# Transposing the attention values of the second mixer: from four TensorE transposes to a write, reads and one VectorE transpose of 32x32 blocks

## The chip, the cores and the metric

The kernel runs on one core of a Trainium2 chip. The metric is the time of one execution on the device in microseconds (us), lower is better. The engines are TensorE (PE in the profile; its weight loads are PEld), VectorE (DVE), ScalarE (ACT), GpSimd (POOL) and SyncE (SP), which only issues transfers. Each has its own queue and works through it in order; they meet at semaphores.

## The reference

The program is a two-layer encoder trunk on 512 tokens of width 1024. Layer 0 has an mLSTM mixer, layer 1 a band attention, and each has a memory attention beside it and a gated channel mixer behind it. The change is in layer 1. What it computes, cut down:

```python
ks_, vs_ = jnp.split(rmsnorm(x, kv_norm_g) @ w_kv, 2, axis=-1)   # 768 + 768 columns
q, q_mem = jnp.split(rmsnorm(x, norm_mix_g[1]) @ b_w_in, [768], axis=-1)
# 12 heads of 64; a chunk of 64 queries sees its own chunk and the 8 before it
s = jnp.einsum('bqhd,bkhd->bhqk', qc, kc) * 64 ** -0.5 + bias     # -inf where not valid
p = jax.nn.softmax(s, axis=-1)
out = jnp.einsum('bhqk,bkhd->bqhd', p, vc)
mem_out = memory_attention(q_mem, mem, mem_w_kv[1])               # 4 heads, 256 memory rows
x = x + jnp.concatenate([out, mem_out], axis=-1) @ b_w_out
```

With 512 tokens (8 chunks) the band of 9 chunks reaches every earlier token, so each query sees all tokens up to the end of its own chunk.

## The kernel before

Activations are held with channels on the 128 partitions and the 512 tokens along the free axis. A float32 product is done as three products of parts: every operand is split into a high part (a copy by ScalarE, L147) and a low part (a subtraction by VectorE, L148), and `mm3` (L203 to L205) adds high by high, high by low and low by high in PSUM.

The twelve heads go in six pairs, and one pair fills the 128 partitions. `project_pair(j)` (L1477) makes what pair j needs. It projects the values, the keys and the queries one after the other (`project`, eight steps of three products each, 24 products of 512 columns). The values and keys are scaled by the row of reciprocal norms (`times_row`, L1480), the queries by L652. The keys go through `head_keys` (L612, L613), the queries through `head_queries` (L602 to L606), where GpSimd clears half of each low part with a memset (L602).

The values are needed the other way round, with tokens on partitions, because they are the stationary operand of the last product of the attention. Before, TensorE transposes the four blocks of 128x128 into one PSUM bank (L1491), and two splits of 128x256 read that bank and write the parts for tokens 0 to 255 and 256 to 511.

`band_attention(j)` then goes through four blocks of 128 queries: scores on TensorE (L622), the sum with the bias and its minimum on VectorE (L1518), exponential on ScalarE (L1522), reciprocal and scaling on VectorE (L1523, L1524), transposes of the probabilities on TensorE (L1533) and their split. At its end come the products with the values (L1554 and L1555).

`weave` emits the steps of the attention of pair j between the steps of the projections of the pairs that come later, at a rate written by hand for each attention, so that TensorE has products to do while a softmax is on its way:

```python
for j in range(4):
    until(lambda: j in qkv, fill)
    weave(band_attention(j, *qkv.pop(j)), fill, (1.68, 1.826, 1.633, 1.848)[j], 4)
```

After pair 3 come the memory attention, pair 4, a second memory attention and pair 5, in the same manner. In other parts of the program the order on TensorE, ScalarE and VectorE is written out by hand. Here it isn't: the framework's planner takes the instructions in the order in which they were emitted as their priority, estimates with its own costs when each could start, and lays down the order of every queue, those of SyncE and GpSimd too. Buffers come from rings with a fixed number of places, and an instruction that writes a new buffer waits until a place is free. The rings that matter are `wr` (3 raw weight tiles, filled by SyncE's loads, L162), `wh0` to `wl2` (3 pairs of split weights), `t` (8 tiles of 128x512, for scaled values, softmax results and the like), `fh` and `fl` (4 each, for the split values of pairs 0 to 4), `u` (50), and in PSUM `mm` (3 banks, for projections and, before, the transposed values), `sc` (3) and `tr` (2).

The last stage of the kernel already turns a tensor in the way that the change does: `load_quadrants` (L1603) reads a stored tensor in pieces so that blocks of 32x32 lie ready, and `token_major` (L1611) transposes these blocks on VectorE.

Of the kernel before, what the change touches and what calls it, by code (L numbers as in the profile page):

```python
# [9 lines left out]
F32 = mybir.dt.float32  # L10
# [6 lines left out]
P = 128  # L17
D = 1024
S = 512
KT = D // P  # L20
TT = S // P
# [27 lines left out]
UNITS = {PLAIN + i: tuple((i, j) for j in range(*LOADS[i][2:])) for i in range(len(LOADS))}  # L49

H = S // 2
ORDERED = {mybir.EngineType.PE, mybir.EngineType.Activation, mybir.EngineType.DVE}


def f(ap):
    return ap.bitcast(F32)
# [3 lines left out]
def trunk(  # L60
# [18 lines left out]
    nc = tc.nc  # L79
    V, A, G = nc.vector, nc.scalar, nc.gpsimd  # L80
# [12 lines left out]
    dram = ctx.enter_context(tc.tile_pool(name="dram", bufs=1, space=bass.MemoryType.DRAM))  # L93

    def sb(tag, shape, dtype=F32):
        count[0] += 1
        return pool.tile(shape, dtype, tag=tag, name=f"{tag}{count[0]}", bufs=bufs[tag])

    def ps(tag):
        count[0] += 1  # L100
        return psum.tile([P, S], F32, tag=tag, name=f"p{tag}{count[0]}", bufs=pbufs[tag])
# [12 lines left out]
    ident = cpool.tile([P, P], F32, name="ident")  # L114
# [31 lines left out]
    def split(hi, lo, src, on_act=True, pinned=False):  # L146
        high = A.copy(hi, src) if on_act else V.tensor_copy(hi, src)  # L147
        low = V.tensor_tensor(out=lo, in0=src, in1=f(hi), op=ALU.subtract)  # L148
        if pinned:
            pin(high)  # L150
            pin(low)
# [42 lines left out]
    def weights(*args):  # L194
        return parts(load(*args))

    def rows(w, c0, n, k0=0, k1=None):
        k1 = k1 if k1 is not None else w.shape[0] // P
        return w[k0 * P : k1 * P, c0 : c0 + n].rearrange("(k p) c -> p k c", p=P)

    def mm3(o, lh, ll, rh, rl, first, last, more=False):

        nc.tensor.matmul(o, lh, rh, start=first, stop=False, skip_group_check=more)  # L203
        nc.tensor.matmul(o, lh, rl, start=False, stop=False, skip_group_check=more)  # L204
        nc.tensor.matmul(o, ll, rh, start=False, stop=last, skip_group_check=more)  # L205

    def project(w, c0, act, tag="mm", parts=None):


        n = len(act)  # L210
        wh, wl = parts or weights(rows(w, c0, P), n, P)
        o = ps(tag)
        for k in range(n):
            mm3(o, wh[:, k, :], wl[:, k, :], act[k][0], act[k][1], k == 0, k == n - 1)
            yield
        return o
# [167 lines left out]
    for k in range(KT):  # L384
        if k % 2 == 0:
            src = mem[:, k * P : (k + 2) * P].rearrange("(m p) c -> p m c", p=P)
# [53 lines left out]
    norm = Norm()  # L440
# [158 lines left out]
    def head_queries(t, scale=1.0):  # L599
        qs, ls = ([sb("u", [P, S], F32R) for _ in range(2)] for _ in range(2))  # L600
        for h, r in enumerate(HEADS):
            G.memset(f(ls[h])[HEADS[1 - h], :], 0.0)  # L602
            A.activation(qs[h][r, :], t[r, :], AF.Copy, scale=scale)
            V.scalar_tensor_tensor(ls[h][r, :], t[r, :], scale, f(qs[h])[r, :], op0=ALU.mult, op1=ALU.subtract)
        for h, r in enumerate(HEADS):
            A.copy(qs[h][HEADS[1 - h], :], f(qs[h])[r, :])  # L606
        return qs, ls

    def head_keys(t):
        ks = [sb("u", [P, S], F32R) for _ in range(2)]  # L610
        for h, r in enumerate(HEADS):
            A.copy(ks[h][r, :], t[r, :])  # L612
            V.tensor_tensor(out=ks[h][HEADS[1 - h], :], in0=t[r, :], in1=f(ks[h])[r, :], op=ALU.subtract)  # L613
        return ks
# [32 lines left out]
    def queries(o, row):  # L647

        if row is None:
            return head_queries(o, HD**-0.5)  # L650
        q = sb("t", [P, S])
        V.scalar_tensor_tensor(q, o, HD**-0.5, row, op0=ALU.mult, op1=ALU.mult)  # L652
        return head_queries(q)
# [89 lines left out]
    class ChannelMixer:  # L743
# [54 lines left out]
        def block_sums(self):  # L798

            self.sums = []  # L800
            for k in range(KT // 2):
# [6 lines left out]
                for o, x, y in (  # L808
                    (ta[:, :H], b1[:, H:], b1[:, :H]),
                    (ta[:, H:], b2[:, H:], ta[:, :H]),  # L810
                    (tb[:, :H], b2[:, H:], b1[:, H:]),
                    (tb[:, H:], b2[:, :H], ta[:, H:]),
                ):
                    V.tensor_tensor(out=o, in0=x, in1=y, op=ALU.subtract)
                yield
                for t in (ta, tb):
                    hi, lo = sb("u", [P, S], F32R), sb("u", [P, S], F32R)
                    split(hi, lo, t)
                    forms += [(hi[:, :H], lo[:, :H]), (hi[:, H:], lo[:, H:])]
                    yield  # L820
# [54 lines left out]
        def products(self, o, w, act, first=False):  # L875

            n = KT // 2
            for k in range(n):
                mm3(o[:, :H], w[0][:, k], w[1][:, k], *act[k], first and k == 0, k == n - 1, True)

# [14 lines left out]
        def tiles(self):  # L895
# [17 lines left out]
            def own_sums():  # L913
                yield
                for part in prep.all_sums():
                    part()
                    yield
# [7 lines left out]
            first = self.forms if self.l else own_sums()  # L925
            with tc.manual_schedule(engines=ORDERED):
                og = run(self.plain_chain(0, False, w[0]))
# [228 lines left out]
    act = acts  # L1156
# [39 lines left out]
    e, u, c, r = (cpool.tile([P, TT, AH], F32, name=f"gate{i}") for i in range(4))  # L1196
# [253 lines left out]
    norm2, kvact, act = Norm(), [], []  # L1450
# [10 lines left out]
    norm = norm2  # L1461
# [15 lines left out]
    def project_pair(j):  # L1477
        def times_row(o):
            t = sb("t", [P, S])
            V.tensor_tensor(out=t, in0=o, in1=norm.row, op=ALU.mult)  # L1480
            return t

        ov = yield from project(w_kv, AW + j * P, kvact)
        t = times_row(ov) if norm.row is not None else None
        o = yield from project(w_kv, j * P, kvact)
        if t is None:
            t = times_row(ov)
        k = head_keys(times_row(o))
        tp = ps("mm")
        for T in range(TT):  # L1490
            nc.tensor.transpose(tp[:, T * P : (T + 1) * P], t[:, T * P : (T + 1) * P], ident)  # L1491
        v = []
        for i in range(2):

            w = sb("u" if j == 5 else ("fh", "fl")[i], [P, S], F32R).rearrange("p (h c) -> p h c", h=4)
            split(w[:, :, :HD], w[:, :, HD:], tp[:, i * MEM : (i + 1) * MEM].rearrange("p (h c) -> p h c", h=4))
            v += [w[:, :2, :], w[:, 2:, :]]
        q = queries((yield from project(b_w_in, j * P, act)), norm.row)
        qkv[j] = q, k, v

    def band_attention(j, q, k, v):
# [88 lines left out]
    for hf in range(2):  # L1590
        G.dma_start(fgb[hf], bass.AP(tensor=final_g.tensor, offset=final_g.offset + hf * S, ap=[[0, P], [1, S]]))
    xt = [[None] * 2 for _ in range(TT)]
    B = 32
    xq = []

    def load_quadrants():

        for hf in range(2):
            xq.append(sb("pt", [P, 5 * S])[:, : 4 * S].rearrange("p (f t) -> p f t", t=P))
            for b in range(4):  # L1600
                block = xspill[4 * hf][:, b * P :]
                src = bass.AP(tensor=block.tensor, offset=block.offset, ap=[[S, B], [B * S, 16], [1, P]])
                tc.keep_in_program_order(nc.sync.dma_start(xq[hf][b * B : (b + 1) * B], src))  # L1603

# [3 lines left out]
    def token_major(T, hf):  # L1608
        xt[T][hf] = sb("u", [P, S])
        block = xq[hf].rearrange("p f (c t) -> p f c t", t=TT)[:, :, :, T]  # L1610
        V.transpose(xt[T][hf].rearrange("p (f c) -> p f c", c=B), block)  # L1611

# [35 lines left out]
    n = LAST // 2  # L1648
# [33 lines left out]
    whole = slice(0, S)  # L1682
    with tc.manual_schedule(engines=ORDERED):
        os_ = [ps(t) for t in ("mm", "mm", "mm", "sc")]
# [93 lines left out]
```

## Time and profile before

| | before |
|---|---|
| median of 3 runs | 1167.95 us (1167.5 to 1168.17) |
| profiled execution, its own time | 1168.55 us |
| span of the profile | 1166.5 us |
| granted clock of TensorE | 0.998 of full speed |
| busy: TensorE, its weight loads | 1156.2 us, 1033.2 us |
| busy: VectorE, ScalarE, GpSimd | 1001.8 us, 747.9 us, 151.2 us |
| the change's stage | about 608 to 798 us of the span |

The span is the time between the first and the last instruction of the profiled execution; the execution's own time has about 2 us around it. Busy time of TensorE counts a product from its start to its modelled end, and products overlap, so the distance between starts says more than a duration. In a row of a timeline the columns are start, duration, engine, line, operation, output and input by tile name, shape and count; a bracket at the end gives how long the engine was idle before it and what ended that. In a row for one line, the three numbers are shortest, median and longest duration in ns. "DMA to landing" is the time from issue to the last byte.

### The profile page before, as it was taken

The numbers are of one execution on the slowest core, as the hardware profiler recorded it, in microseconds if no ns is written. First come the engines' busy times: TensorE is split into PE (matmuls) and PEld (weight loads), VectorE is DVE, ScalarE is ACT, GpSimd is POOL, SyncE is SP. The second block draws the span as 40 slices with busy tenths as digits, with TensorE's granted clock in tenths as the row PEclk, the third lists the DMA queues.
The fourth block names the chain that finished last, engine by engine and source line by source line (L and its number), as shares of the span: only waits on it lengthen the run. The fifth ranks groups of instructions, "written<-read, shape, count | busy, mean of one in ns | idle before, by whom it ended". The sixth has DMA issues, their size and how long they took to land.

```text
span 1166.5 us, 19282 instructions
## 1 busy us (share of the span) xinstructions
PE 1156.2 (99%) x7189; PEld 1033.2 (89%) x7189; DVE 1001.8 (86%) x1781; ACT 747.9 (64%) x1343; POOL 151.2 (13%) x254
## 2 busy tenths in 40 slices
PE   9999999999999999999999999999999999999997
PEld 9988888888999999999888888778899999999986
DVE  6877688779999988888797888898999998889977
ACT  6548677657776655555575667776776665555654
POOL 1211101000122222111021000100010111111100
PEclk9999999999999999999999999999999999999999
DMA  8745325244468878777564322335445767777682
GB/s 282 230 110 134 96 56 153 66 134 140 139 157 182 213 178 195 182 173 162 147 193 133 91 62 63 122 107 157 142 126 143 174 146 180 172 180 174 143 157 78
DMA packets 207855, 171.26 MB, mean 147 GB/s; under 512 B 9256, under 2 KB 182030, under 8 KB 207762
## 3 DMA queue, kind: packets, MB, share of 16 engines
q1 hardware_dynamic: 188018, 123.93, 37.1%
q0 software_dynamic: 19168, 45.06, 19.3%
q8 instruction: 56, 0.92, 0.3%
q10 hardware_dynamic: 576, 1.05, 0.2%
q14 instruction: 37, 0.30, 0.1%
HBM read 133.09 MB, written 40.85 MB: 149 GB/s over the span
## 4 chain that ended last, share of the span: by engine, by line
PE 96%; DVE 2%; ACT 1%; DMA 0%; issue 0%; POOL 0%; POOLq 0%; DVEq 0%
PE pmm L203 19%; PE pmm L204 18%; PE pmm L205 18%; PE ptr L204 6%; PE ptr L203 6%; PE ptr L205 6%; PE psc L203 5%; PE psc L204 5%; PE psc L205 5%; PE psc L622 2%; PE ptr L1533 1%; PE ptr L1554 1%; PE ptr L1555 1%; PE ptr L691 1%; PE pmm L513 0%; PE ptr L705 0%
## 5 line engine op out<-in xcount | busy, mean ns | idle before, releaser
L203 PE MATMUL pmm<-u,wh 128*128 128x256 f32 (+1 forms) x992 | 334.9, 338 | 0.1
L205 PE MATMUL pmm<-u,wl 128*128 128x256 f32 (+1 forms) x992 | 332.1, 335 | 0.0
L204 PE MATMUL pmm<-u,wh 128*128 128x256 f32 (+1 forms) x992 | 331.9, 335 | 0.0
L148 DVE TENSOR_TENSOR wl<-wr,wh 128x1024 fp32r<-128x1024 f32 (+4 forms) x165 | 184.8, 1120 | 56.0 <-ACT wh L147 55.4
L205 PEld LDWEIGHTS pmm<-u,wl 128*128 128x128 f32 x992 | 186.3, 188 | 18.9
L203 PEld LDWEIGHTS pmm<-u,wh 128*128 128x128 f32 x992 | 186.4, 188 | 16.7 <-ACT u L147 0.9
L204 PEld LDWEIGHTS pmm<-u,wh 128*128 128x128 f32 x992 | 186.5, 188 | 16.2 <-DVE u L148 0.5
L147 ACT CAST wh<-wr 128x1024 fp32r<-128x1024 f32 (+4 forms) x165 | 159.6, 970 | 62.5 <-PE pmm L204 30.1
L203 PE MATMUL ptr<-u,wh 128*128 128x512 f32 x272 | 106.5, 392 | 0.0
L204 PE MATMUL ptr<-u,wh 128*128 128x512 f32 x272 | 106.3, 391 | 0.0
L205 PE MATMUL ptr<-u,wl 128*128 128x512 f32 x272 | 105.8, 389 | 0.0
L147 ACT CAST fh<-pt 128x512 fp32r<-128x512 f32 x120 | 74.8, 625 | 34.5 <-DVE pt L1059 33.2
L203 PE MATMUL pmm<-u,fh 128*128 128x256 f32 x320 | 88.8, 278 | 0.0
L205 PE MATMUL pmm<-u,fl 128*128 128x256 f32 x320 | 88.6, 277 | 0.0
L204 PE MATMUL pmm<-u,fh 128*128 128x256 f32 x320 | 88.5, 276 | 0.0
L981 ACT COPY t<-pmm 128x256 f32<-128x256 f32 x120 | 45.0, 375 | 67.3 <-PE pmm L205 67.2
L148 DVE TENSOR_TENSOR fl<-pt,fh 128x512 fp32r<-128x512 f32 x120 | 82.3, 687 | 3.1
L765 DVE SCALAR_TENSOR_TENSOR t<-t,cols,t 128x511 f32<-128x511 f32 x88 | 65.9, 749 | 7.3 <-ACT t L772 5.8
L203 PE MATMUL psc<-u,wh 128*128 128x256 f32 (+1 forms) x208 | 63.2, 304 | 0.0
L205 PE MATMUL psc<-u,wl 128*128 128x256 f32 (+1 forms) x208 | 62.9, 302 | 0.0
L204 PE MATMUL psc<-u,wh 128*128 128x256 f32 (+1 forms) x208 | 62.9, 302 | 0.0
L203 PEld LDWEIGHTS pmm<-u,fh 128*128 128x128 f32 x320 | 60.1, 188 | 2.2 <-ACT t L981 0.7
(359 smaller groups left out, 2642.0 us busy)
## 6 DMA issues: line engine op xcount, KB each, us to landing
wr<-in_ffn_w_up_dram SPq DMA_DIRECT2D x46, 512.0 KB, 8.5
pt<-in_ffn_w_up_dram SPq DMA_DIRECT2D x40, 512.0 KB, 8.3
wr<-in_ffn_w_down_dram SPq DMA_DIRECT2D x32, 512.0 KB, 5.4
wr<-in_a_w_in_dram SPq DMA_DIRECT2D x20, 512.0 KB, 3.8
xspill<-bias POOLq DMA_DIRECT2D x32, 256.0 KB, 7.0
without_row<-bias POOLq DMA_DIRECT2D x24, 256.0 KB, 4.1
wr<-in_w_kv_dram SPq DMA_DIRECT2D x12, 512.0 KB, 4.0
without_row<-t POOLq DMA_DIRECT2D x24, 256.0 KB, 4.1
```

Source lines behind the costliest of these rows:

```text
L147: high = A.copy(hi, src) if on_act else V.tensor_copy(hi, src)
L148: low = V.tensor_tensor(out=lo, in0=src, in1=f(hi), op=ALU.subtract)
L203: nc.tensor.matmul(o, lh, rh, start=first, stop=False, skip_group_check=more)
L204: nc.tensor.matmul(o, lh, rl, start=False, stop=False, skip_group_check=more)
L205: nc.tensor.matmul(o, ll, rh, start=False, stop=last, skip_group_check=more)
L622: nc.tensor.matmul(o, a, b, start=first and i == 0, stop=i == 1)
L691: nc.tensor.transpose(tp[:, a, i, :], es[T2, h][:, i, a * P : (a + 1) * P], ident)
L765: V.scalar_tensor_tensor(acc[:, n:], src[:, : S - n], self.fw[:, c * FT + j : c * FT + j + 1], acc[:, n:], op0=ALU.mult, op1=ALU.add,)
L981: A.copy(o, r[:, :H])
L1533: nc.tensor.transpose(tp[:, b * P : (b + 1) * P], es[T, h][:, b * P : (b + 1) * P], ident)
L1554: nc.tensor.matmul(o2[:, s * P :], w, hi_at(pts[h], s, s, TT - s), start=s == 0, stop=False)
L1555: nc.tensor.matmul(o2[:, s * P :], w, lo_at(pts[h], s, s, TT - s), start=False, stop=s == TT - 1)
```

## The change

The scaled values `t` of pair j are written by GpSimd to a tensor of their own in DRAM, with partition 32a + b going to row 4b + a. After the keys and the queries are emitted, SyncE reads that tensor back in four transfers, one for each group of 32 tokens out of every 128. Such a transfer fills 32 partitions: partition b holds, for each a and each block T of 128 tokens, the 32 values of channel 32a + b, so a piece is 32 numbers, 128 bytes. One instruction of VectorE transposes all the 32x32 blocks and orders them so that tokens lie on the partitions and channels along the free axis. The two splits read this tile in SBUF, and no longer a PSUM bank. They, the reads and the transpose are now emitted after the projection of the queries and not before it. The tiles `r` and `tp` come from the ring `t`; the four TensorE transposes and their bank from `mm` are gone.

```diff
@@ project_pair(j)
         o = yield from project(w_kv, j * P, kvact)
         if t is None:
             t = times_row(ov)
+        vt = dram.tile([P, S], F32, name=f"values{j}")
+        rows4 = bass.AP(tensor=vt.tensor, offset=vt.offset, ap=[[S, 4], [4 * S, B], [1, S]])
+        G.dma_start(rows4, t)
         k = head_keys(times_row(o))
-        tp = ps("mm")
-        for T in range(TT):
-            nc.tensor.transpose(tp[:, T * P : (T + 1) * P], t[:, T * P : (T + 1) * P], ident)
+        q = queries((yield from project(b_w_in, j * P, act)), norm.row)
+        r, tp = sb("t", [P, S]), sb("t", [P, S])
+        for b in range(4):
+            block = vt[:, b * B :]
+            src = bass.AP(tensor=block.tensor, offset=block.offset, ap=[[4 * S, B], [P, 16], [1, B]])
+            nc.sync.dma_start(r[b * B : (b + 1) * B].rearrange("p (n c) -> p n c", c=B), src)
+        V.transpose(
+            tp.rearrange("p (T a c) -> p a T c", T=TT, a=4), r.rearrange("p (a T c) -> p a T c", T=TT, a=4)
+        )
         v = []
         for i in range(2):
             w = sb("u" if j == 5 else ("fh", "fl")[i], [P, S], F32R).rearrange("p (h c) -> p h c", h=4)
             split(w[:, :, :HD], w[:, :, HD:], tp[:, i * MEM : (i + 1) * MEM].rearrange("p (h c) -> p h c", h=4))
             v += [w[:, :2, :], w[:, 2:, :]]
-        q = queries((yield from project(b_w_in, j * P, act)), norm.row)
         qkv[j] = q, k, v
```

`B` is 32; its definition moves to the head of the file, with no other effect.

2 lines of the change are left out of this document (1 added, 1 removed).

## The prediction

> **What bounds the kernel now.** I read the page first, then the windows of the second mixer, then single rows of it.
>
> ```profile
> span 1166.5 us, 19282 instructions
> ...
> PE 1156.2 (99%) x7189; PEld 1033.2 (89%) x7189; DVE 1001.8 (86%) x1781; ACT 747.9 (64%) x1343; POOL 151.2 (13%) x254
> ...
> PE 96%; DVE 2%; ACT 1%; DMA 0%; issue 0%; POOL 0%; POOLq 0%; DVEq 0%
> ```
>
> TensorE is busy for 99% of the span and holds 96% of the chain that ended last, so an instruction taken off TensorE shortens the end unless it makes TensorE wait. VectorE at 86% is the next engine, and it gets the new work. The shares by stage (time, then TensorE matmul, weight load, VectorE, ScalarE, GpSimd, clock, DMA share, GB/s) for the stage that the change touches, cut at the starts of the bands:
>
> ```profile
> 608.40:628.90 20.50, 20.50 (x93) 16.83 (x92) 15.51 (x21) 12.19 (x19) 4.72 (x9) 1.00 0.51 160
> 628.90:653.55 24.65, 24.54 (x129) 20.73 (x128) 21.75 (x56) 16.45 (x39) 2.19 (x4) 1.00 0.31 86
> 653.55:678.80 25.25, 25.25 (x133) 21.09 (x131) 21.53 (x56) 16.63 (x39) 2.30 (x4) 1.00 0.31 88
> 678.80:703.50 24.70, 24.70 (x131) 20.66 (x129) 20.98 (x56) 16.89 (x39) 0.00 (x0) 1.00 0.21 63
> 703.50:738.00 34.50, 34.50 (x174) 28.58 (x173) 27.11 (x65) 23.01 (x49) 3.12 (x6) 1.00 0.34 106
> 738.00:758.50 20.50, 19.78 (x106) 15.79 (x106) 19.54 (x50) 15.44 (x43) 3.13 (x6) 1.00 0.26 80
> 758.50:798.40 39.90, 39.60 (x217) 32.07 (x216) 35.66 (x100) 29.03 (x76) 1.09 (x2) 1.00 0.36 104
> ```
>
> Up to 738 us TensorE idles 0.11 us in all, and VectorE idles 2.9 to 7.4 us in each window. From 738 to 758.5 VectorE idles only 0.96 us and TensorE 0.72 us: there the two are close to joint bounds. The granted clock is 1.00 throughout, so it enters no term.
>
> **Removed: 24 transposes on TensorE, four for each pair of heads.** Their row, and the order of TensorE around the first four:
>
> ```profile
> L1491 PE MATMUL pmm<-ident,t x24: 270/272/273, 619.6 to 744.6; 128*128 128x128 f32 x24
> ...
> 619.12 0.39 PE L204 MATMUL pmm<-u,wh 128*128 128x512 f32 x1
> 619.35 0.39 PE L205 MATMUL pmm<-u,wl 128*128 128x512 f32 x1
> 619.58 0.60 PE L1491 MATMUL pmm<-ident,t 128*128 128x128 f32 x4
> 619.93 0.48 PE L203 MATMUL pmm<-u,wh 128*128 128x512 f32 x1
> 620.25 0.40 PE L204 MATMUL pmm<-u,wh 128*128 128x512 f32 x1
> ```
>
> Starts of products are 0.23 us apart (619.12 to 619.35). Without the four transposes L203 would start at 619.58 and L204 at 619.81; it starts at 620.25, so four transposes cost 0.44 us of the line, not four times 272 ns, since they are pipelined. The gain is 6 x 0.44 = 2.64 us. Its ends: 6 x 0.35 = 2.10 (619.58 to 619.93, the shift of the first start) and 6 x 0.60 = 3.60 (the four as busy time). I take 0.44, which counts the whole delay of the following stream.
>
> The bank of PSUM that the transposes filled comes free as well. With 0.11 us of idle on TensorE before 738 there is nothing for it to repair: 0.
>
> **Added on VectorE: one transpose of 32x32 blocks per pair, 128x512.** The kernel has that instruction in its last stage:
>
> ```profile
> L1611 DVE STREAM_TRANSPOSE u<-pt x8: 1042/1070/1099, 1135.3 to 1146.8; 128x512 f32<-128x512 f32 x8
> ```
>
> So 6 x 1.07 = 6.42 us more on VectorE. What covers it is idle time there. The next windows run, for pairs 1, 2 and 5, from the start of the value projection's scaling (L1480) to about the end of the splits of its transposed values:
>
> ```profile
> 632.20:645.90 13.70, 13.59 (x75) 11.44 (x74) 12.92 (x35) 9.75 (x23) 2.19 (x4) 1.00 0.29 78
> 656.84:671.00 14.16, 14.16 (x75) 11.54 (x74) 13.20 (x35) 9.36 (x22) 2.30 (x4) 1.00 0.37 104
> 740.00:752.00 12.00, 11.61 (x64) 9.00 (x62) 11.76 (x26) 9.11 (x25) 3.12 (x6) 1.00 0.29 97
> ```
>
> In these stretches VectorE idles 0.78, 0.96 and 0.24 us: no room for 1.07. Outside them there is: in band 0, 24.65 - 21.75 - 0.78 = 2.12 us. The question is whether the transpose may wait until then. The rows of the values of pair 1 and of single gaps:
>
> ```profile
> 632.20 0.69 DVE L1480 TENSOR_TENSOR t<-pmm,rb 128x512 f32<-128x512 f32 x1
> 642.34 0.41 DVE L148 TENSOR_TENSOR fh<-pmm,fh 128x256 fp32r<-128x256 f32 x1
> 672.90 0.68 DVE L642 TENSOR_TENSOR t<-ptr,t 64x512 f32<-64x512 f32 x1 [1.27 <-ACT t L641]
> 682.48 1.23 DVE L148 TENSOR_TENSOR wl<-wr,wh 128x1024 fp32r<-128x1024 f32 x1 [1.77 <-ACT wh L147]
> 735.94 1.23 DVE L148 TENSOR_TENSOR wl<-wr,wh 128x1024 fp32r<-128x1024 f32 x1 [3.00 <-ACT wh L147]
> ...
> 670.76 0.50 PE L1554 MATMUL ptr<-pt,fh 128*128 128x512 f32 x1
> ```
>
> The values of pair 1 are scaled at 632.20, split from 642.34, and first used by L1554 at 670.76: 28 us of slack after the split began. The edit also emits transpose and splits after the query projection, so in the planner's order they stand behind work that is due sooner. A gap of 1.27 to 3.00 us holds the transpose whole. I therefore take 0 for pairs 0 to 4 (ends: 0, and 5 x 1.07 = 5.35 if every gap turns out to be needed). For pair 5, in 738 to 758.5, the ends are -0.44 (hidden, gain kept) and +1.07 (all on the line); with 0.96 us idle against 1.07 I take the middle, +0.3, in place of that pair's gain.
>
> The two splits per pair keep their engines and size; only their source moves from PSUM to SBUF. ScalarE's half in either case, in the same shape:
>
> ```profile
> L147 ACT CAST fl<-pmm x5: 372/372/373, 623.8 to 720.2; 128x256 fp32r<-128x256 f32 x5
> L147 ACT CAST u<-wr x2: 400/404/408, 727.4 to 727.7; 128x256 fp32r<-128x256 f32 x2
> ```
>
> That is 32 ns more each, and ScalarE idles 8 us a band: 0.
>
> The Trainium skill (VectorE: DVE Perf Modes, The three transpose paths) gives 390 ns for a 128x128 TensorE transpose in bf16 and 311 ns for VectorE's blocks. Taken at 390 ns each, the 24 would be an estimated 9.4 us; the rows' 0.11 us per transpose decides instead.
>
> **Added on GpSimd and SyncE: six writes and 24 reads.** The nearest rows, first a write of 256 KB from GpSimd with its landing, then the eight reads of the last stage, each 512 pieces of 512 B:
>
> ```profile
> L1460 POOL DMA_DIRECT2D xspill<-fl x4: 539/540/542, 597.1 to 609.4; - x4
> DMA to landing us min/median/max: 2.3/2.5/3.5
> ...
> L1603 SPq DMA_DIRECT2D pt<-xspill x8: 346/858/1706, 1122.4 to 1128.9; - x8
> DMA to landing us min/median/max: 6.4/8.2/8.8
> ...
> wr<-in_w_kv_dram SPq DMA_DIRECT2D x12, 512.0 KB, 4.0
> rep<-maskf POOLq DMA_DIRECT2D x12, 16.0 KB, 3.3
> ```
>
> A new read has 512 pieces of 128 B; none of that size is in the trace. By count of pieces the four reads of a pair (2,048) are half of those eight (4,096); a weight load has 1,024 and lands in 4.0 us, and the small-piece row (64 rows of 256 B) in 3.3. So landing lies between 3.3 and 8.8 us; I take 6.4, the fastest of the like-shaped reads. For pair 1: scaled by 632.9, issue 0.54, write landed 2.5, four issues 4 x 0.37 = 1.5 (a single one in SyncE's rows below), landing 6.4: 643.8. The ends are 632.9 + 0.54 + 2.3 + 1.4 + 3.3 = 640.4 and 632.9 + 0.54 + 3.5 + 6.8 + 8.8 = 652.5. All lie 18 us or more ahead of 670.76.
>
> The queues that these steps stand in:
>
> ```profile
> 634.51 12.96 SPq L162 DMA_DIRECT2D wr<-in_w_kv_dram  x2
> 652.47 0.37 SPq L162 DMA_DIRECT2D wr<-in_b_w_in_dram  x1
> ...
> 637.35 1.15 POOL L602 MEMSET u<- 64x512 f32 x2 [23.08 <-ACT t L1522]
> 662.86 1.10 POOL L602 MEMSET u<- 64x512 f32 x2 [22.69 <-PE psc L622]
> ```
>
> On SyncE the reads wait for the write to land, and weight loads queue behind them. A load fills one of three raw buffers as soon as a split frees it and is itself split three projections later, at least 3 x 24 x 0.23 = 16.6 us, of which it takes 4.0; SyncE waits some 12 us between the two loads of the first row. A hold of 3.5 + 1.5 us is covered: 0; without that cover it would be those 5 us a pair. On GpSimd the write waits for the scaled values, and memsets and bias reads queue behind; GpSimd idles 23 us at a time: 0. If the write stood behind the memset of 662.86 instead, it would issue near 664, and 2.5 + 1.5 + 6.4 + 1.07 + 0.8 (two splits of 0.41) brings the values at 676.3, 5.5 us after 670.76; a planner that orders by readiness puts it ahead, so I price it at 0 too.
>
> Two more buffers of the ring t (8) are held for a while per pair, while the old one comes free when the write has landed. Ends: 0, and one step on a tile of that size late, 0.69 us per pair as in L1480's row; I take 0.
>
> **Sum.** 5 x (-0.44) + 0.3 = -1.9 us. The profiled execution took 1168.55 us (2.05 around its span), 0.60 over the median of the runs shown, 1167.95. The forecast is 1168.55 - 1.9 = 1166.65 for such an execution and 1166.05, say 1166.0, for the median. Its own range is -3.6 (0.60 each) to -0.7 (5 x 0.35 less, 1.07 more): 1164.4 to 1167.3.
>
> **Rivals.**
> - *VectorE becomes the bound.* For it: the 93% or more in the three short windows, and 95% in 738 to 758.5. Against it: gaps of 1.27 to 3.00 us at the ends of the bands in which it waits for others. Price: all 6.42 on the line less 2.64, +3.8: 1171.7.
> - *VectorE stands at the head of its queue waiting for pieces (slower).* Place: the transpose, if it is ordered before its reads have landed; behind it stand that band's softmax steps, on which TensorE's transposes (L1533) wait. At the old place of the splits (642.34) the wait would be 1.5 us by my landing and up to 10.2 by the late end. A band hides 2.12 us, so with a wait w a pair loses 1.07 + w - 2.12 and gains 0.44: it decides from w = 1.5. At w = 3, about half of the middle between those ends, since the order has much room after 642, 6 x 1.51 = +9: 1177. For it: 128-byte pieces are new and the planner's guess of them is not visible; against it: the room.
> - *Nothing is gained*: the freed 0.44 us is taken up by waits of TensorE for softmax results, because filler products run out sooner. For it: the stage is dense on both engines. Against it: TensorE idles 0.11 us before 738. Time: 1167.95.
>
> The Trainium skill (DMA: Bandwidth & Descriptors, Specifications) sets 512 B as the least transfer for line rate and says that smaller ones are done by read-modify-write. By that rule the reads would land toward the late end and the second rival would hold; no transfer of 128-byte pieces has been seen here.
>
> **How the numbers follow.** Forecast 0.48, VectorE as bound 0.20, late pieces 0.15, nothing gained 0.17. A measurement of this kernel tells 0.2% (2.3 us) from no change. The forecast's own range lies on both sides of -2.3: 0.30 of its 0.48 I give to faster, as 0.44 per pair kept in all six is already -2.64; the rest and the nothing-gained case are the same, 0.35; the other two are slower, 0.35. The range goes from 1164.4 to 1174, which takes in VectorE as the bound and late pieces up to w = 2.5, and leaves out the rest of that case and a small part below.
>
> **What would show it.** Right: L1491 gone, matmul starts 0.23 us apart across its places, the transposes of VectorE in gaps after the old splits with no wait on DMA before them, splits done before L1554. Wrong: idle time of VectorE before its transpose that a DMA ends; TensorE idling over 1.2 us in the stage, on L148 or L1524; landings over 10 us; SyncE's weight loads late for ScalarE's L147. A stage before 738 that is longer than before makes the prediction wrong even where the total falls.

## The result and the profile after

The changed kernel takes 1171.62 us (median of 7 runs, 1171.46 to 1171.97) against 1167.98 us (7 runs, 1167.5 to 1168.38) for the kernel before: ratio 1.0032, 95% interval 1.002 to 1.0044. It is slower by 3.6 us, where 1.9 us less had been forecast. The profiled execution took 1171.97 us.

The page of the changed kernel (engine busy time with its share, number of instructions, then the shares of the chain that ended last):

```profile
span 1170.3 us, 19303 instructions
...
PE 1156.5 (99%) x7165; PEld 1031.1 (88%) x7165; DVE 1001.7 (86%) x1787; ACT 749.1 (64%) x1343; POOL 155.5 (13%) x260
...
PE 92%; DVE 4%; ACT 3%; issue 1%; DMA 0%; POOL 0%; DVEq 0%; POOLq 0%
```

TensorE runs 24 instructions fewer (7189 to 7165), as the change says, and yet the span grew by 3.8 us. TensorE's share of the chain fell from 96% to 92%; VectorE and ScalarE took it over. So TensorE now waits where it did not wait. Where, is seen from two products that both programs issue in the same place, one ahead of the stage and one behind it. Timeline rows of TensorE (start, duration, engine, line, operation, tiles, shape, count), before:

```profile
608.40 0.39 PE L204 MATMUL pmm<-u,wh 128*128 128x512 f32 x1
...
830.34 0.62 PE L307 MATMUL psc<-t,onesr 128*128 128x512 f32 x2
```

and after (lines are one higher there):

```profile
608.39 0.39 PE L205 MATMUL pmm<-u,wh 128*128 128x512 f32 x1
...
834.30 0.62 PE L308 MATMUL psc<-t,onesr 128*128 128x512 f32 x2
```

The two kernels are level at 608 us and 3.96 us apart at 830 us. The whole loss is made in the stage of the change; I call this difference the stage's shift (830.34 to 834.30, less the -0.01 at its start) and give it for the experiments too. Windows (time, then busy time of TensorE, weight load, VectorE, ScalarE, GpSimd with instruction counts, clock, DMA share, GB/s) show where in the stage TensorE stands idle. The two windows before:

```profile
750.00:780.00 30.00, 29.38 (x159) 23.71 (x159) 27.68 (x76) 22.74 (x61) 1.09 (x2) 1.00 0.36 106
780.00:810.00 30.00, 30.00 (x152) 24.62 (x151) 24.59 (x62) 19.98 (x42) 1.09 (x2) 1.00 0.37 108
```

and five after:

```profile
630.00:660.00 30.00, 29.80 (x148) 24.16 (x148) 24.07 (x63) 18.88 (x43) 2.85 (x5) 1.00 0.49 120
660.00:690.00 30.00, 29.76 (x151) 24.29 (x150) 23.59 (x69) 19.35 (x46) 2.84 (x5) 1.00 0.37 101
...
720.00:750.00 30.00, 29.58 (x155) 23.84 (x154) 27.74 (x56) 22.77 (x52) 6.35 (x12) 1.00 0.48 126
750.00:780.00 30.00, 28.68 (x152) 23.69 (x150) 28.05 (x73) 24.22 (x57) 1.09 (x2) 1.00 0.38 106
780.00:810.00 30.00, 27.55 (x142) 21.82 (x141) 23.29 (x67) 19.23 (x47) 0.00 (x0) 1.00 0.41 119
```

Up to 750 us TensorE idles 0.2 to 0.4 us in each of the windows shown. In the last two it idles 1.32 and 2.45 us, against 0.62 and 0 before. The rows of that stretch with idle time before them (bracket: how long, and what ended it):

```profile
779.43 0.33 PE L623 MATMUL psc<-u,u 128*128 128x128 f32 x1 [1.09 <-ACT t L680]
785.97 2.11 PE L706 MATMUL ptr<-pt,u 128*128 128x512 f32 x8 [1.14 <-DVE pt L149]
788.76 0.51 PE L623 MATMUL psc<-u,u 128*128 128x256 f32 x2 [0.68 <-DVE s L1527]
789.87 0.62 PE L623 MATMUL psc<-u,u 128*128 128x384 f32 x2 [0.60 <-DVE s L1527]
```

These are waits on softmax work of the memory attention and of pair 5, 3.51 us in four rows. Between the two products shown above, TensorE's idle time grew from 1.13 to 5.05 us. Its busy time stayed at 220.8 and 220.9 us, although 24 instructions are gone, so the gain of 2.64 us is lost too, in longer distances between its products. Why the attention is late there is seen 150 us earlier, at the first softmax step of each band (the sum of scores and bias, L1518 before, L1527 after). VectorE before:

```profile
629.27 0.29 DVE L1518 CUSTOM_DVE_ANT_0 t<-psc,bias 128x128 f32<-128x128 f32 x1 [0.17 <-PE psc L622]
```

VectorE after:

```profile
627.18 1.39 DVE L605 SCALAR_TENSOR_TENSOR u<-t,u 64x512 fp32r<-64x512 f32 x2
632.28 1.23 DVE L149 TENSOR_TENSOR wl<-wr,wh 128x1024 fp32r<-128x1024 f32 x1 [3.71 <-ACT wh L148]
633.42 0.70 DVE L1499 STREAM_TRANSPOSE t<-t 128x512 f32<-128x512 f32 x1
634.05 0.25 DVE L1527 CUSTOM_DVE_ANT_0 t<-psc,bias 128x128 f32<-128x128 f32 x1
...
712.84 0.70 DVE L1499 STREAM_TRANSPOSE t<-t 128x512 f32<-128x512 f32 x1
713.47 0.25 DVE L1527 CUSTOM_DVE_ANT_0 t<-psc,bias 128x128 f32<-128x128 f32 x1
```

Before, the step followed the scores within 0.17 us. After, VectorE's queue holds ahead of it the low part of a weight split, which waits 3.71 us for ScalarE's high part, and then the new transpose. Band 0 starts 4.8 us late (629.27 to 634.05). The pair "transpose, first softmax step" stands in this order in bands 0 to 3, and they start 4.8, 4.8, 5.0 and 9.7 us late. The wait for ScalarE on the weight split ahead of it is 3.71, 1.54, 0.26 and 3.23 us in the four bands, so part of the delay of the later bands is carried over from the earlier ones. TensorE did not fall behind at once, since it had projection products to run ahead with. An estimate from the trace's rows shows it: with each product other than the removed transposes counted at the median distance to the next start for its form (0.23 us for 512 columns), TensorE is 0.7 us ahead of the kernel before at 738 us, 2.2 us ahead at 775, and 2.8 us behind at 790. It loses this lead from about 775 us on, presumably because the products to run ahead with are used up there.

The new operations themselves, by their lines (the numbers are shortest, median and longest in ns; then first and last start), after:

```profile
L1491 POOL DMA_DIRECT2D values<-t x6: 704/726/747, 620.3 to 744.5; - x6
...
DMA to landing us min/median/max: 6.7/7.2/8.2
...
L1498 SPq DMA_DIRECT2D t<-values x24: 544/619/971, 628.5 to 759.6; - x24
...
DMA to landing us min/median/max: 2.4/3.6/4.2
...
L1499 DVE STREAM_TRANSPOSE t<-t x6: 702/704/712, 633.4 to 764.1; 128x512 f32<-128x512 f32 x6
```

The write takes 7.2 us to land where 2.5 was reckoned; the reads take 3.6 where 6.4 was; the transpose 0.70 where 1.07 was. No DMA ends an idle time of VectorE ahead of it here. In band 0 that is a near thing: the last pieces landed at 633.1 us, 0.3 us before the transpose started, so without the weight split VectorE would have waited for them instead.

### The profile page after: what moved, and what is told of

Same layout as the page of the kernel before. It is cut to its first block, busy times and chain, and to the rows that moved or that the text cites. A ratio compares the mean times of both kernels' runs of the same rounds, so it can differ in the third digit from the quotient of the medians.

```text
span 1170.3 us, 19303 instructions
## 1 busy us (share of the span) xinstructions
PE 1156.5 (99%) x7165; PEld 1031.1 (88%) x7165; DVE 1001.7 (86%) x1787; ACT 749.1 (64%) x1343; POOL 155.5 (13%) x260
## 4 chain that ended last, share of the span: by engine, by line
PE 92%; DVE 4%; ACT 3%; issue 1%; DMA 0%; POOL 0%; DVEq 0%; POOLq 0%
PE pmm L204 18%; PE pmm L206 17%; PE pmm L205 17%; PE ptr L205 6%; PE ptr L204 6%; PE ptr L206 6%; PE psc L205 5%; PE psc L204 5%; PE psc L206 5%; PE psc L623 2%; PE ptr L1542 1%; ACT u L607 1%; DVE t L643 1%; ACT wh L148 1%; ACT u L604 1%
## 5 line engine op out<-in xcount | busy, mean ns | idle before, releaser
L149 DVE TENSOR_TENSOR u<-t,u 128x512 fp32r<-128x512 f32 (+1 forms) x80 | 56.5, 712 | 7.3 <-ACT u L148 6.8
```

## The experiments

The shift in the last column comes from one profiled execution of each kernel, which lies up to 1.2 us from that kernel's median; the medians decide.

| run | what differs from the changed kernel | median us | kernel before | ratio, 95% interval | stage's shift us |
|---|---|---|---|---|---|
| changed kernel | | 1171.62 | 1167.98 | 1.0032, 1.002 to 1.0044 | +3.97 |
| e1_bias_first | bias reads earlier | 1172.21 | 1168.03 | 1.0034, 1.0022 to 1.0047 | +4.5 |
| e2_write4 | write in four | 1172.09 | 1168.03 | 1.0033, 1.0021 to 1.0046 | +5.8 |
| e3_old_pair0 | pair 0 as before | 1173.83 | 1168.03 | 1.005, 1.0037 to 1.0062 | +6.6 |
| e7_no_dma | no write, no reads | 1167.93 | 1168.03 | 1.0, 0.9991 to 1.0009 | +0.2 |
| e8_other_ring | r, tp from ring rb | 1172.79 | 1168.34 | 1.0038, 1.0025 to 1.0051 | +5.0 |
| e8b_other_ring_write4 | ring rb, write in four | 1167.22 | 1168.34 | 0.9991, 0.9982 to 1.0 | -0.5 |
| e9_later | reads and transpose inside the band | 1190.82 | 1168.34 | 1.0193, 1.0179 to 1.0207 | +22.3 |
| e5_order_only | TensorE's transposes, at the later place | 1169.86 | 1168.34 | 1.0013, 1.0004 to 1.0022 | +1.8 |
| e10_early_place | ring rb, write in four, early place | 1167.08 | 1168.43 | 0.9988, 0.998 to 0.9997 | -1.0 |
| e11_early_ring_t | write in four, early place | 1171.16 | 1168.43 | 1.0023, 1.0014 to 1.0032 | +3.1 |
| e12_ring_write_bias | ring rb, write in four, bias earlier | 1167.02 | 1168.43 | 0.9988, 0.9979 to 0.9997 | -0.7 |
| e13_no_transpose | no transpose of any kind | 1165.73 | 1168.42 | 0.9977, 0.9967 to 0.9986 | -2.3 |

**The bias reads.** On GpSimd's queue the write stands ahead of the two bias reads of the pair, whose landing rose from 3.6 to 6.7 us. The edit puts them at the head of `project_pair`:

```diff
     def project_pair(j):
...
+        load_bias(j)
         ov = yield from project(w_kv, AW + j * P, kvact)
```

> The changed kernel with one move: the two bias reads of pair j are emitted at the head of project_pair(j), so that on GpSimd they no longer stand behind the write of the values. Theory B (bias): in the changed kernel the bias reads of band 0 are issued at 622.1 us in place of 611.0 and land at 631 to 632, so the first softmax of band 0 on VectorE comes at 634 in place of 629, every band stays 4 to 5 us late and TensorE has no filler left at 778 to 790 us. It expects the first L1527 near 629 and about 1166 us (1171.6 less some 5). Theory W (wait on pieces): VectorE's transpose stands ahead of that softmax and its pieces land at 633, so the bias does not decide: first L1527 still at 633 to 635 and 1171 to 1172 us.

The first softmax step of band 0 stays where it was; VectorE's timeline has it behind the same two instructions:

```profile
631.88 1.23 DVE L149 TENSOR_TENSOR wl<-wr,wh 128x1024 fp32r<-128x1024 f32 x1 [3.70 <-ACT wh L148]
633.14 0.71 DVE L1511 STREAM_TRANSPOSE t<-t 128x512 f32<-128x512 f32 x1
633.78 0.25 DVE L1534 CUSTOM_DVE_ANT_0 t<-psc,bias 128x128 f32<-128x128 f32 x1
```

The late biases are not what sets the start, and theory B falls.

**The slow write.** Its rows are grouped by four (slowest dimension 4); split into four writes, each has 32 rows as its slowest dimension:

```diff
-        rows4 = bass.AP(tensor=vt.tensor, offset=vt.offset, ap=[[S, 4], [4 * S, B], [1, S]])
-        G.dma_start(rows4, t)
+        for a in range(4):
+            rows = vt[a : a + 1, :]
+            every = bass.AP(tensor=rows.tensor, offset=rows.offset, ap=[[4 * S, B], [1, S]])
+            G.dma_start(every, t[a * B : (a + 1) * B])
```

> The changed kernel with the write of the values split into four writes of 32 partitions each, to the same places. Measured in the changed kernel: one write lands 6.7 to 8.2 us after issue, where the writes of the activations with the same bytes land in 2.3 to 3.5. If the pattern with a slowest dimension of 4 spreads the write over only a few DMA engines, each of the four lands in 2.5 to 4 us and the reads are issued 3 to 5 us sooner; if the place (DRAM rows of 2 KB) is slow by itself, landing stays at 7. Theory W expects the pieces of pair 0 by 629 and about 1167 us. Theory B expects bias reads landing near 627 and so a gain too, to 1167 to 1169. A theory in which VectorE's added work decides expects 1171 to 1172.

The writes by their line:

```profile
L1493 POOL DMA_DIRECT2D values<-t x24: 498/498/593, 618.4 to 745.7; - x24
...
DMA to landing us min/median/max: 1.9/2.0/2.6
```

and VectorE's timeline at the start of band 0:

```profile
631.76 1.23 DVE L149 TENSOR_TENSOR wl<-wr,wh 128x1024 fp32r<-128x1024 f32 x1 [3.69 <-ACT wh L148]
632.91 0.70 DVE L1501 STREAM_TRANSPOSE t<-t 128x512 f32<-128x512 f32 x1
633.54 0.25 DVE L1529 CUSTOM_DVE_ANT_0 t<-psc,bias 128x128 f32<-128x128 f32 x1
```

Each quarter lands in 2.0 us, and all 256 KB within 3.3 to 3.4 us of the first issue, where the one write took 7.2 us. So the form of the write was slow, not the place it goes to. The Trainium skill (DMA: Bandwidth & Descriptors, Why a DMA increments its semaphore by 16 and not by 1) says that a transfer is spread over the largest number of engines, up to 16, that divides the slowest dimension of both sides; that would be 4 for the one write and 16 for each of the four, and the trace's 7.2 against 2.0 us agrees. The time does not fall, though: the order on VectorE is as before, and the transpose, whose pieces now arrive in time (the last of pair 0 at 629.2 us), still stands behind the weight split, and the softmax behind the transpose. Theory W, by which the pieces alone set the start, expected 1167 us and falls in this form.

**Pair 0 alone.** The first pair goes back to TensorE's transposes at their old place, the other five stay:

```diff
+        new = j > 0
...
+        if not new:
+            tp = ps("mm")
+            for T in range(TT):
+                nc.tensor.transpose(tp[:, T * P : (T + 1) * P], t[:, T * P : (T + 1) * P], ident)
```

> The changed kernel with pair 0 done as before (TensorE transposes ahead of the query projection), pairs 1 to 5 as changed. Theories B and W place the whole loss at the start of band 0, where the values of pair 0 have no band to hide under: both expect the first L1527 near 629 us and a total of 1168 - 5 x 0.44 = about 1165.8 us. The theory that VectorE's load in all bands costs the time expects five sixths of it back at most: 1171 us.

Band 0 is on time again (628.9), and band 1 is late as in the changed kernel, for the same cause, as VectorE's timeline shows:

```profile
656.50 1.23 DVE L149 TENSOR_TENSOR wl<-wr,wh 128x1024 fp32r<-128x1024 f32 x1 [3.71 <-ACT wh L148]
657.64 0.70 DVE L1512 STREAM_TRANSPOSE t<-t 128x512 f32<-128x512 f32 x1
658.27 0.25 DVE L1540 CUSTOM_DVE_ANT_0 t<-psc,bias 128x128 f32<-128x128 f32 x1
```

So the loss is not one event in band 0, where both theories had placed it: with pair 0 as before, pair 1 makes it. That this mixture is 2 us slower than the full change is not explained by these rows and stays open.

**Without the transfers.** The VectorE transpose reads the scaled values themselves, and the kernel leaves out the regrouping through DRAM:

```diff
-        r, tp = sb("t", [P, S]), sb("t", [P, S])
-        for b in range(4):
-            block = vt[:, b * B :]
...
+        r, tp = t, sb("t", [P, S])
```

> The changed kernel without its write and reads: VectorE transposes the blocks of the scaled values themselves, in the same place of the program. It leaves out the regrouping through DRAM, so the values of the attention stand in the wrong places. TensorE's transposes are gone and VectorE's are there, so it measures VectorE's added work alone. If that work decides: 1170 to 1172 us. If transfers decide (B or W): 1165 to 1166 us.

All bands start on time (629.0, 653.5, 678.9, 703.2 us) and the loss is gone, so it comes with the transfers, not with VectorE's extra 4.2 us (6 x 0.70). `tp` is still a tile of ring t here, but with nothing to wait for its transpose of pair 0 runs at 625.1 us, ahead of the softmax. But the 2.64 us of the removed transposes aren't gained either.

**The ring.** In every kernel so far with transfers, the first softmax result, a tile of ring t, is written directly behind tp, a tile of ring t emitted ahead of it. Here r and tp come from ring rb, whose three tiles of the same size hold rows of norms:

```diff
-        r, tp = sb("t", [P, S]), sb("t", [P, S])
+        r, tp = sb("rb", [P, S]), sb("rb", [P, S])
```

> The changed kernel with r and tp taken from the ring rb (3 tiles of the same size, of which the norm row holds one in this stage) in place of the ring t; nothing else. Theory R: tiles of one ring are handed out in the order of emission, so a softmax result of band j (ring t) can't be written before tp of pair j is, that is not before its pieces have landed; that puts the transpose, and a weight split before it, ahead of the band's first softmax on VectorE. It expects the first L1527 of bands 0 to 3 at their times of before (629, 654, 679, 704 us, within 1 us), no starved TensorE at 778 to 790, and 1168 us, like the run without transfers. Rival O: the transpose stands there only because it was emitted earlier; the ring changes nothing: 1171.5 to 1172.5 and first L1527 at 634.

VectorE's timeline:

```profile
629.13 0.29 DVE L1527 CUSTOM_DVE_ANT_0 t<-psc,bias 128x128 f32<-128x128 f32 x1 [0.17 <-PE psc L623]
...
632.57 0.71 DVE L1499 STREAM_TRANSPOSE rb<-rb 128x512 f32<-128x512 f32 x1 [3.15 <-DMA rb<-values]
```

and the rows of TensorE's timeline that have idle time before them:

```profile
633.78 0.33 PE L1542 MATMUL ptr<-ident,t 128*128 128x128 f32 x1 [1.77 <-DVE t L1533]
635.52 0.47 PE L1542 MATMUL ptr<-ident,t 128*128 128x128 f32 x1 [0.94 <-DVE t L1533]
```

In band 0 the order changed as the theory says: softmax first, at its old time. The 1168 us that it expected did not come. Now the transpose follows at once, and VectorE stands 3.15 us at the head of its queue waiting for the pieces (4.9 us in three places over the six pairs), and TensorE waits for the softmax behind it. Bands 1 to 3 start 3.8, 3.8 and 4.5 us late. The planner presumably set the transpose where it reckoned the pieces to be there (its estimate is not visible); with the write at 7.2 us they are not.

A ring with no free place would hold the softmax back too, but ring t wasn't full. In the changed kernel the last tile of the norm is read at 617.9 us, and after it only five of the eight places are asked for ahead of band 0: the values, the keys, the queries, r and tp. The first three are done with by 628.6 us, so when the scores are ready near 629 us r and tp are the only ones held.

**Ring and write together.** The two edits above in one kernel:

> As the run with the other ring, and the write in four parts (landing 2.0 us in place of 7.2). In the order of the other-ring kernel the transpose of pair 0 stands right behind the first softmax step of band 0, where its pieces (landed at 632 to 633 with the one write, at 629 with four) would hold VectorE some 3 us. Theory R expects 1167 to 1168, up to 1 us under the other-ring run; rival O no difference from 1172.

VectorE's timeline, the writes by their line, and the last window:

```profile
628.76 0.29 DVE L1529 CUSTOM_DVE_ANT_0 t<-psc,bias 128x128 f32<-128x128 f32 x1 [0.17 <-PE psc L623]
...
631.34 0.71 DVE L1501 STREAM_TRANSPOSE rb<-rb 128x512 f32<-128x512 f32 x1
631.98 0.31 DVE L1535 TENSOR_SCALAR t<-t,s 128x256 f32<-128x256 f32 x1
```

```profile
L1493 POOL DMA_DIRECT2D values<-t x24: 496/499/541, 618.9 to 741.4; - x24
...
DMA to landing us min/median/max: 1.9/2.0/4.1
```

```profile
780.00:810.00 30.00, 29.81 (x146) 24.16 (x145) 24.28 (x63) 19.09 (x42) 1.41 (x3) 1.00 0.39 110
```

1167.22 us: neither edit gains anything alone (1172.09 and 1172.79), together they take off 4.9 and 5.6 us. The transpose lies among the softmax steps and waits for nothing, and TensorE's idle time at 780 to 810 us falls from 2.45 to 0.19 us. Bands 0 to 3 start at 628.8, 653.1, 678.0 and 703.5 us, none later than before; with ring t and the write in four they are 4.3, 4.3, 4.5 and 9.2 us late. This is the cause of the loss: the order that ring t brings, and the slow write, either of which is enough to make bands late.

**The place.** Two runs move the new work. In the first, reads, transpose and splits go into the band, behind the second block's softmax:

```diff
-        qkv[j] = q, k, v
+        qkv[j] = q, k, token_rows
...
         yield from softmax(1)
+        v = v()
         yield from transposed(0)
```

> The changed kernel with the reads, the transpose and the splits of pair j emitted inside its band, after the second softmax block, still from the ring t. Theory R: the first two blocks of the band get their tiles first, so the first L1527 comes at 629, 654, 679, 704 us; the third block then stands behind tp, but by that time the pieces have long landed: 1167.5 to 1169. Rival O expects the same here. A theory in which VectorE's added transposes decide by themselves expects no better than the run without transfers, 1168.

It costs 22 us, where theory R and rival O both expected 1167.5 to 1169. A band's first softmax step no longer stands behind the transpose, but the next tile of ring t does, the scaling of the next values (L1481), and TensorE waits for that. VectorE's timeline in band 2, then TensorE's:

```profile
699.84 0.70 DVE L1501 STREAM_TRANSPOSE t<-t 128x512 f32<-128x512 f32 x1
700.47 0.65 DVE L1481 TENSOR_TENSOR t<-pmm,rb 128x512 f32<-128x512 f32 x1
```

```profile
701.17 0.50 PE L204 MATMUL pmm<-u,wh 128*128 128x512 f32 x1 [3.37 <-DVE t L1481]
```

This wait comes twice, 6.7 us of the 17.8 us that TensorE idles in the stage. The reads of pair 1 go out at 661.6 us instead of 648.8, but those of pair 0 at 628.3, as in the changed kernel (628.5). What makes up the rest of the 22 us was not separated. The second run is the kernel before with only the later place of the emission: TensorE's transposes and the splits behind the query projection.

```diff
-        tp = ps("mm")
-        for T in range(TT):
-            nc.tensor.transpose(tp[:, T * P : (T + 1) * P], t[:, T * P : (T + 1) * P], ident)
...
         q = queries((yield from project(b_w_in, j * P, act)), norm.row)
+        tp = ps("mm")
+        for T in range(TT):
+            nc.tensor.transpose(tp[:, T * P : (T + 1) * P], t[:, T * P : (T + 1) * P], ident)
```

> The kernel before with one part of the change alone: the TensorE transposes and the splits of the values are emitted after the query projection and not before it. No write, no reads, no VectorE transpose. If the later place alone disturbs the bands it is 1169 or more and the first L1519 later than 630; theory R expects 1167.5 to 1168.5, since the four transposes wait for no transfer and their bank comes from another ring.

1.5 us slower by the medians (1169.86 against 1168.34), a shift of 1.8 us in the stage. That is 0.13%, under the bound of 0.2%, and so a hint only. If it held for the new form as well, putting it back would gain as much. The next two kernels ask that, with the write in four and with ring rb, then ring t:

```diff
-        q = queries((yield from project(b_w_in, j * P, act)), norm.row)
         r, tp = sb("rb", [P, S]), sb("rb", [P, S])
...
+        q = queries((yield from project(b_w_in, j * P, act)), norm.row)
         qkv[j] = q, k, v
```

> The changed kernel with the other ring and the write in four, as in the run before that came to 1167.22 us, and with reads, VectorE transpose and splits emitted at once behind the write, ahead of the query projection, where the TensorE transposes stood before. Theory R (hand-out order of the ring, plus the slow write, plus 1.8 us for the later place of the emission): the place is given back, so 1165.4 to 1166.4 us, and the band starts stay within 1 us of before. Rival W: emitted earlier, the transposes stand ahead of work that could run on VectorE and wait there for their pieces (write 2.0 + reads 3.6 us); then VectorE rows of the transpose show idle time released by a DMA of about 3 us, as with the other ring alone, and the time is 1169 to 1173 us. Rival N: the place counts only for TensorE's transposes, 1167.2 us as with the late place.

> As the run with the early place, four writes, but r and tp from ring t as in the changed kernel. Theory R: ring t hands its tiles out in the order of emission, so the first softmax step still can't pass the transpose; but the pieces are asked for about 8 us earlier, so the transpose can be done before the band starts: band starts within 1.5 us of before, 1166 to 1169 us. Rival: the ring costs what it costs wherever the transposes are emitted, because other tiles of ring t then wait behind it in their turn: 1171 to 1174 us.

With ring rb the place makes no difference that can be told (1167.08 and 1167.22). If the later place costs anything, it does so with TensorE's transposes, and why was not measured. With ring t the early place saves little (1171.16), and I had expected it to mend the order. VectorE's rows show that another tile of ring t now stands behind the transpose:

```profile
630.92 1.23 DVE L149 TENSOR_TENSOR wl<-wr,wh 128x1024 fp32r<-128x1024 f32 x1 [4.21 <-ACT wh L148]
632.06 0.70 DVE L1500 STREAM_TRANSPOSE t<-t 128x512 f32<-128x512 f32 x1
632.69 0.65 DVE L653 SCALAR_TENSOR_TENSOR t<-pmm,rb 128x512 f32<-128x512 f32 x1
...
635.87 0.29 DVE L1529 CUSTOM_DVE_ANT_0 t<-psc,bias 128x128 f32<-128x128 f32 x1 [0.39 <-PE psc L623]
```

L653 is the scaling of the queries. It is held until 632.69 (it ran at 625.63 in the kernel with ring rb), the scores with it, and the softmax comes at 635.87. So in the three places tried, the next tile of ring t stands behind the transpose; only which tile that is changes.

**Best found, and the ceiling.** Ring rb, write in four, and the bias reads early, three edits that are shown above:

> Other ring, write in four, late place, and the bias reads of a pair moved ahead of its value projection, so that they no longer stand behind the write on GpSimd's queue. Theory R: with the ring and the write mended the bias is no longer late by enough to matter: 1166.5 to 1168 us, the same as 1167.22. Theory B (the bias reads are the rest of the loss): 1165 to 1166 us and the band starts earlier than in the run without the move.

1167.02 us, the lowest of the kernels that compute the whole reference, and not told apart from 1167.22 and 1167.08. Against the kernel before it is 0.1% faster (0.9979 to 0.9997), too little to call a gain at the bound of 0.2%. Last, a kernel that leaves out the turning of the values: the splits read the scaled values with no transpose at all:

```diff
-        tp = ps("mm")
-        for T in range(TT):
-            nc.tensor.transpose(tp[:, T * P : (T + 1) * P], t[:, T * P : (T + 1) * P], ident)
+        tp = t
```

> The kernel before without the 24 TensorE transposes and with nothing in their place: the splits read the pair's values as they are, so the second mixer multiplies values in the wrong places. Its time is the ceiling of what the change can bring. If the sum of the prediction holds (24 transposes of 0.11 us on the path), 1165.3 to 1165.9 us. If the attention chain rather than TensorE's own work sets the end of this stage, the ceiling is lower: 1166.5 to 1168 us, and then the best kernels here (1167.02 to 1167.22) have all there is to have.

The page of this kernel:

```profile
span 1163.8 us, 19230 instructions
...
PE 1153.4 (99%) x7165; PEld 1030.5 (89%) x7165; DVE 1000.6 (86%) x1781; ACT 748.1 (64%) x1343; POOL 151.7 (13%) x254
```

2.7 us less than before (1168.42 to 1165.73). The 24 transposes are worth what the prediction's sum said. By the medians the best version keeps 1.4 of these 2.7 us (1168.43 to 1167.02). What takes the other 1.3 us (VectorE's transposes, the transfers, or the order that the planner makes of them) was not separated.

## Why the prediction was wrong

Two steps of the sum failed, and either alone is enough for the loss. The first is the one on the ring: "Two more buffers of the ring t (8) are held for a while per pair ... Ends: 0, and one step on a tile of that size late, 0.69 us per pair ...; I take 0." With the write in four, ring t against ring rb is 1172.09 against 1167.22 us (4.9 us, 0.8 per pair), outside even the upper end. The price was looked for in a place that comes free late. What the ring did instead was to set an order: the next tile of ring t to be written stands behind tp. That the framework hands out a ring in the order of emission is my reading of it; the runs show the order in the kernels with ring t and transfers, and its absence with ring rb.

The second is the wait for the pieces, put at nothing because they land 18 us or more ahead of their first use by L1554. What counted was not that use but the softmax, which stands behind the transpose in VectorE's queue. The write took 7.2 us to land where 2.5 was taken; with ring rb, the slow write against the write in four is 1172.79 against 1167.22 us (5.6 us). The reads were faster than taken, so for pair 0 the way from the write's issue to the last piece is 12.8 us (620.3 to 633.1), not far from the 10.9 us of the prediction: the size alone would not have shown the wait. In the changed kernel it is the order that shows, because the weight split holds VectorE until 0.3 us after the pieces have landed; mending the ring alone brings nothing (1172.79 against 1171.62).

Point by point:

- *Removed, -2.64 us.* Right: -2.7 us with nothing in their place.
- *The transpose on VectorE, 1.07 us, hidden.* The size was too high, 0.70 us. That VectorE has room for it without a wait was right in the kernel with ring rb and the write in four (631.34). "In the planner's order they stand behind work that is due sooner" was wrong with ring t: the work due sooner, the softmax, stood behind it. The prediction read gaps in VectorE's time and took it that the transpose may use any of them; the queue is worked through in order, and ring t decided its place.
- *The write, 2.5 us.* Mis-sized: 7.2 us. The row used as its price writes 128 rows in one pattern; this one goes in four groups. With the write in four and the ring as it is, the time stays at 1172.09: each of the two failed steps is hidden behind the other.
- *The reads, 6.4 us, bounds 3.3 to 8.8.* 3.6 us, near the lower end. What the prediction drew from the Trainium skill (DMA: Bandwidth & Descriptors, Specifications), that pieces under 512 B would land toward the late end, did not come. What the Trainium skill states is about line rate, and that these reads do not contradict: 64 KB in 3.6 us is far less per us than a weight load's 512 KB in 4.0.
- *The queues of SyncE and GpSimd, 0.* On GpSimd the biases took 3 us longer to land, and the first was issued at 622.1 us instead of 611.0. With the bands late anyway this cost nothing that can be told (1172.21 with them early). SyncE's hold shows in no row that TensorE waits for.
- *Rival: VectorE becomes the bound, 1171.7.* The number is met and the mechanism is not: VectorE's busy time on the page is 1001.7 us against 1001.8, and the kernels that carry the same six transposes in ring rb take 1167 us.
- *Rival: VectorE stands waiting for pieces, 1177.* Its mechanism and place are what ring rb alone shows in band 0 (3.15 us at the head of the queue, TensorE's L1542 waiting), at a lower price, +4.5 us (1168.34 to 1172.79): VectorE waits ahead of three of the six transposes, 4.9 us together. In the changed kernel itself VectorE stood for ScalarE's weight split, and the transpose was only in the way.
- *Rival: nothing gained.* That is about what the change gives without the transfers (1167.93).
- *The signs to look for.* TensorE idle over 1.2 us in the stage was the right sign. "A stage before 738 that is longer" was the wrong place: products ahead of time covered the delay there, and the bill came at 775 to 790 us. The sign that a DMA ends VectorE's idle time ahead of its transpose did not show in the changed kernel, though the late pieces are half of the cause. The range, 1164.4 to 1174.0, held the time, but the case that it held near 1171.7, VectorE as the bound, is not the one measured, so that is luck.

## What to carry to other kernels

Whoever moves a step to another engine should list the in-order queues and the rings that its tiles join: a tile that waits for a transfer, taken from a ring that latency-critical results use, can put those results behind the transfer, whatever gaps the engine has. Delay in a chain that another engine runs ahead of is paid where that engine's filler ends, so the start times of the chain, not the idle time nearby, are to be compared. And two causes that each suffice hide one another: each mended alone brought nothing, both together took about 5 us off.

## What the runs showed of the hardware

A write of 256 KB from GpSimd landed in 7.2 us as four groups of 32 rows. As four writes of 64 KB it landed in 2.0 us each, 3.3 to 3.4 us in all, at 0.50 us of issue for each instead of 0.73. In the changed kernel, reads of 512 pieces of 128 B landed in 2.4 to 4.2 us, and each held SyncE's queue for 0.62 us instead of the 0.37 of a weight load. VectorE's block transpose of 128x512 took 0.70 us here and 1.07 us in the last stage of the kernel; the operation and the size are the same, the access patterns are not (the last stage reads every fourth value of a row), and what makes the difference was not measured.
